# Dilated attention on one core: group sums and weights cross the token orders by way of DRAM, scores and units in pairs

## The chip, the cores and the metric

The kernel runs on one core of a Trainium2 chip. The metric is the time of one execution in microseconds (us), as the device tells it; a run gives the median of its repetitions. TensorE (PE in the profile; PEld is its loading of weights), VectorE (DVE), ScalarE (ACT), GpSimd (POOL) and SyncE (SP) each run their own queue of instructions in order, and wait for one another at semaphores.

## The reference

Two transformer blocks follow each other on 512 tokens of width 1024. The change lies in the second block's first mixer, a dilated attention with 16 heads of 64. Each head attends three times (windows and dilations 128/1, 512/4, 2048/16), and the three results are mixed by a softmax over their log-sums. Cut to what matters:

```python
for g, (window, dilation) in enumerate(DILATED_PATTERNS):     # ((128,1),(512,4),(2048,16))
    q = rotary(proj[:, :, g, 0], pos)
    k = rotary(proj[:, :, g, 1], pos)
    o, lse = dilated_window_attention(q, k, proj[:, :, g, 2], window, dilation)
    outs.append(o); lses.append(lse)
wts = softmax(stack(lses), axis=0)
o = einsum('gbsh,gbshe->bshe', wts, stack(outs))
return o.reshape(B, S, H * E) @ w_out

# in dilated_window_attention, per block of queries
s = where(valid, einsum(q, k) * E**-0.5, -inf)
m = max(s); p = exp(s - m); l = sum(p)
o = einsum(p / l, v); lse = m + log(l)
```

## The kernel before, in words

The weights come as one stream of 328 tiles of 128 x 1024 (`wst`). `Stream` loads a tile on SP's queue (line 170), and splits it into a high part `whi` on ACT (183) and a low part `wlo` on DVE (184); every projection is three fp32r matmuls (260 to 262, or 370 to 372). Loads run two tiles ahead of the splits, splits four tiles ahead of the use.

The attention `attn` works on head pairs `hp`, 0 to 7. `proj(hp)` is a generator that projects q, k and v of one head pair; `att(hp)` is a generator that attends. The loop at its end takes one step of `att(hp-1)` behind each step of `proj(hp)`, so the order of every engine's queue is this interleaving: **a step** in this text is a piece of projection (12 matmuls of 512 columns, or 24 of 256) and the piece of attention behind it. An even `hp` has 20 projection steps, an odd one 16. What `att` has left when `proj` is through follows without projection between. `att(7)` runs beside the output projection `proj_group0`, with two steps of attention to each of its later steps.

Within `att`, before the change: steps 1 to 4 compute scores (657, into PSUM banks named `dn`, of which there are four), each followed by `soft`: maximum with mask on DVE (637), exponential on ACT (641). Group 0 keeps tokens in order, 128 to a block; groups 1 and 2 keep them by residue (token 4p + r). So sums `ML` of group 0 have to change order before the weights `E` of the three groups can be formed: step 5 does that with 16 small fp32 matmuls against the identity (669) and a copy into `ml` (671), and then forms `E` (674 to 685). Step 8 takes group 0's weights back with 16 matmuls against a constant `back` (744) into `c0`. The first two units' probabilities are scaled in step 7. Steps 9 to 17 run over eight **units** (two score blocks of both heads each): transposes on PE (711, 713), a copy of them from PSUM to `PT` (546 on ACT and 548 on DVE, in turns), scaling by weights of the unit two further on (701 for groups 1 and 2, 704 for group 0, both DVE), and the products with v (734) of the unit before. fp32 matmuls of scores, products and weights appear as two records each.

`rots` holds the rotary's second half of each q/k: POOL issues four DMAs that swap rows (585) and multiplies (592); `fin` on DVE multiplies and adds (595, 596) some steps later. POOL's next DMAs wait for `fin` to be through with the buffers `qks` and `qka`, of which there is one each. In the table below "odd" and "even" are the head pair that is projected meanwhile.

Of the kernel before, what the change touches and what calls it, by code (L numbers as in the profile page):

```python
# [26 lines left out]
F32 = mybir.dt.float32  # L27
# [4 lines left out]
OP = mybir.AluOpType  # L32
PSUM = bass.MemoryType.PSUM

S, D = 512, 1024
# [193 lines left out]
class Kern:  # L229
# [287 lines left out]
    def attn(self, ctx):  # L517
        K, nc, tc = self, self.nc, self.tc
        mm = nc.tensor.matmul
        xT = self.xT  # L520
        inner = ExitStack()
        pool = inner.enter_context(tc.tile_pool(name="attn", bufs=1))

        def const(name, shape):
            t = pool.tile(shape, F32, name=name)
            nc.gpsimd.dma_start(t, K.ins["c_" + name])
            return t

        rot = const("rot", [128, 2, S])
        mask0 = const("mask0", [128, 256])  # L530
        mask1 = const("mask1", [128, 128])
        mask2 = const("mask2", [128, 128])
        back = const("back", [128, 4, 128])
        blk = const("blk", [128, 4])
        x_d = self.dr.tile([128, 4, D], F32, name="x_d")
        for tb in range(4):
            nc.gpsimd.dma_start(x_d[:, tb, :], K.x[:, tb, :])
        oT = K.xp.tile([128, 8, S], F32, name="x")
        hT = [None]
        V0, V12, QT = {}, {}, {}  # L540
# [87 lines left out]
        def att(hp):  # L628
            P0 = pool.tile([128, 4, 2, 256], F32, name="P0")
            P12 = [None, pool.tile([128, 4, 2, 128], F32, name="P1"), pool.tile([128, 4, 2, 128], F32, name="P2")]  # L630
            ML = pool.tile([128, 3, 4, 2, 2], F32, name="ML", bufs=2)
# [3 lines left out]
            def soft(items, sl):  # L635
                for s, mk, dst, idx in items:
                    nc.vector.tensor_tensor_reduce(dst, s, mk, op0=OP.add, op1=OP.max, scale=1.0, scalar=-3e38,
                                                   accum_out=M[idx])
                nc.vector.tensor_scalar(NM[sl], M[sl], -0.125, None, op0=OP.mult)
                for s, mk, dst, idx in items:  # L640
                    nc.scalar.activation(dst, dst, AF.Exp, bias=NM[idx], scale=0.125, accum_out=L[idx])  # L641

            A = slice(None)
            for g, t0 in ((0, 0), (0, 2), (1, 0), (2, 0)):
                q = QT[hp, g]
                its = []
                n = 4 if g else 2
                ps = [K.bank("dn", (128, n, 512 // n)) for _ in range(2)]
                for u in range(n):
                    t = t0 + u  # L650
                    c = slice(t * 128, t * 128 + 128)
                    k0 = 128 if g == 0 and t == 0 else 0
                    keys = c if g else slice((t - 1) * 128 + k0, (t + 1) * 128)
                    for h in range(2):
                        r = slice(64 * h, 64 * h + 64)
                        s = ps[h][:, u, k0:]
                        mm(s, q[r, 0, c], q[r, 1, keys], start=True, stop=True)  # L657
                        its.append((s, (mask0, mask1, mask2)[g][:, k0:], (P0, P12[1], P12[2])[g][:, t, h, k0:],
                                    (A, g, t, slice(h, h + 1))))
                soft(its, (A, g, slice(t0, t0 + n)))  # L660
                yield
            for g in range(3):
                del QT[hp, g]

            p = K.bank("dn")
            pv = p[:, 0:16].rearrange("p (r c h) -> p r c h", r=4, c=2)
            for r in range(4):
                for b in range(4):
                    mm(pv[32 * b:32 * b + 32, r], K.ident[:, r:128:4], ML[:, 0, b], start=True, stop=True)
            ml = pool.tile([128, 4, 2, 2], F32, name="ml", bufs=2)  # L670
            nc.vector.tensor_copy(ml, pv)
            E = pool.tile([128, 3, 4, 2], F32, name="E", bufs=2)
            mx = pool.tile([128, 4, 2], F32, name="mx", bufs=2)
            nc.vector.tensor_tensor(mx, M[:, 1], M[:, 2], op=OP.max)
# [8 lines left out]
            nc.vector.tensor_add(mx, mx, T[:, 2])  # L683
            nc.vector.reciprocal(mx, mx)
            nc.vector.tensor_mul(E, E, mx[:, None].to_broadcast([128, 3, 4, 2]))
            Eb = pool.tile([128, 4, 4, 2], F32, name="Eb", bufs=2)
            nc.vector.tensor_mul(Eb, E[:, 0, :, None, :].to_broadcast([128, 4, 4, 2]),
                                 blk[:, None, :, None].to_broadcast([128, 4, 4, 2]))
            units = [(g, t2) for g in (1, 2) for t2 in range(2)] + [(0, b) for b in range(4)]
            c0 = pool.tile([128, 4, 2], F32, name="c0", bufs=2)  # L690
            yield
            yield
            po = K.bank("o")
            PT = {}

            def scale(g, t):
                for h in range(2):
                    if g:
                        for u in (2 * t, 2 * t + 1):
                            s = P12[g][:, u, h, :]  # L700
                            nc.vector.tensor_scalar(s, s, E[:, g, u, h:h + 1], None, op0=OP.mult)
                    else:
                        s = P0[:, t, h, (128 if t == 0 else 0):256]
                        nc.vector.tensor_scalar(s, s, c0[:, t, h:h + 1], None, op0=OP.mult)

            def tr(g, t):
                p = K.bank("dn", (128, 2, 2, 128))
                for u in range(2):
                    for h in range(2):
                        if g:  # L710
                            nc.tensor.transpose(p[:, u, h, :], P12[g][:, 2 * t + u, h, :], K.ident)  # L711
                        elif t or u:
                            nc.tensor.transpose(p[:, u, h, :], P0[:, t, h, u * 128:u * 128 + 128], K.ident)  # L713
                d = pool.tile([128, 2, 2, 128], F32, name="PT", bufs=3)
                u0 = 1 if (g, t) == (0, 0) else 0
                evac(d[:, u0:2], p[:, u0:2])
                PT[g, t] = d
# [3 lines left out]
            def pv_(g, t):  # L721
                d = PT.pop((g, t))
                for u in range(2):
                    if (g, t, u) == (0, 0, 0):
                        continue
                    for h in range(2):
                        if g:
                            c = slice(2 * t + u, S, 4)
                            v = V12[hp][:, 2 * t + u, (g - 1) * 128 + 64 * h:(g - 1) * 128 + 64 * h + 64]
                        else:  # L730
                            c = slice(t * 128, t * 128 + 128)
                            o = (2 * (hp % 2) + h) * 64
                            v = V0[hp // 2][:, t - 1 + u, o:o + 64]
                        mm(po[64 * h:64 * h + 64, c], v, d[:, u, h, :], start=nth[h] == 0, stop=False,  # L734
                           skip_group_check=True)
                        nth[h] += 1

            scale(*units[0])
            scale(*units[1])
            yield  # L740
            pb = K.bank("dn")
            for k in range(4):
                for r in range(4):
                    mm(pb[32 * k:32 * k + 32, 0:8], back[:, r, 32 * k:32 * k + 32], Eb[:, r].rearrange("p b h -> p (b h)"),  # L744
                       start=r == 0, stop=r == 3)
            nc.vector.tensor_copy(c0, pb[:, 0:8].rearrange("p (b h) -> p b h", b=4))
            yield
            for n in range(len(units) + 1):
                if n < len(units):
                    tr(*units[n])  # L750
                if n + 2 < len(units):
                    scale(*units[n + 2])
                if n:
                    pv_(*units[n - 1])
                yield
            if hT[0] is None:
                nc.scalar.activation(oT[:, hp, :], po, AF.Copy)
            else:
                K.split_ps(hT[0][0][:, hp, :], hT[0][1][:, hp, :], po)
# [57 lines left out]
    def mix(self, ctx):  # L817
# [966 lines left out]
def layout(a, stages):  # L1784
    a = {k: np.asarray(v) for k, v in a.items()}
    d = {"x": np.ascontiguousarray(a["x"][0])}
# [13 lines left out]
    d["c_back"] = np.ascontiguousarray(np.stack([j == 4 * (i % 32) + r for r in range(4)], 1).astype(np.float32))  # L1800
    d["c_blk"] = (i // 32 == np.arange(4)[None]).astype(np.float32)
# [51 lines left out]
```

## Time and profile before

| | us |
|---|---|
| times of three runs | 2183.8, 2183.39, 2186.86 (median 2183.8) |
| the profiled execution's own time | 2180.92 |
| its span, first to last instruction | 2179.2 |
| PE busy (share of span) | 2102.1 (96%) |
| PE weight loads busy | 1758.0 (81%) |
| DVE busy | 1223.5 (56%) |
| ACT busy | 794.0 (36%) |
| POOL busy | 272.3 (12%) |
| dilated attention, head pairs 1 to 7 beside `att` | about 690 to 1195 |

The span is one execution seen by the hardware profiler; 1.7 us of its time lie outside. The engines' busy times overlap, and matmuls are pipelined: one of 512 columns is shown 0.39 us long, yet the next begins 0.23 us after it. So what a piece costs PE is read from starts: from the start of the last projection matmul ahead of it to the start of the second one behind it, less two projection intervals. In the stretch 690 to 1110 PE is shown busy throughout, at full granted clock.

### The profile page before, as it was taken

How to read it: one execution, taken by the hardware profiler on the slowest of the kernel's cores; microseconds unless marked ns; L12 is line 12 of the kernel's file. 1: busy time of each engine (PE TensorE's matmuls, PEld its weight loads, DVE VectorE, ACT ScalarE, POOL GpSimd, SP SyncE). 2: the span in 40 equal slices, each digit the busy share in tenths (PEclk: the TensorE clock that was granted, in tenths of full speed). 3: DMA queues.
4: the chain of work that ended last, by engine and by line, in shares of the span. 5: the costliest groups of instructions: out<-in, count | busy, mean ns of one | idle time of the engine just before them, and what ended most of it. 6: DMA issues, size and time to landing. Idle time of an engine off the chain costs nothing.

```text
span 2179.2 us, 31391 instructions
## 1 busy us (share of the span) xinstructions
PE 2102.1 (96%) x12708; PEld 1758.0 (81%) x12708; DVE 1223.5 (56%) x2153; ACT 794.0 (36%) x1470; POOL 272.3 (12%) x327
## 2 busy tenths in 40 slices
PE   5889899999999999999999999999999999999997
PEld 5877698888888888888887988888898878888885
DVE  6876443333466666657766744444556556444444
ACT  5446333222233444333344432223254534322331
POOL 3740100000012222122220100000100001000001
PEclk9999999999999999999999999999999999999998
DMA  3201232222325333333332222223222222222221
GB/s 126 80 23 47 109 126 97 97 90 85 116 102 170 101 100 111 107 96 109 99 116 101 100 100 97 87 87 106 97 91 78 86 78 80 96 96 90 104 97 68
DMA packets 65026, 209.49 MB, mean 96 GB/s; under 512 B 10544, under 2 KB 15312, under 8 KB 64880
## 3 DMA queue, kind: packets, MB, share of 16 engines
q1 hardware_dynamic: 55808, 180.93, 24.1%
q0 software_dynamic: 6928, 20.09, 3.3%
q10 hardware_dynamic: 2144, 6.45, 0.9%
q8 instruction: 100, 1.64, 0.3%
q14 instruction: 46, 0.38, 0.1%
HBM read 186.46 MB, written 4.19 MB: 87 GB/s over the span
## 4 chain that ended last, share of the span: by engine, by line
PE 59%; issue 24%; DVE 2%; POOL 1%; ACT 1%; DMA 0%; POOLq 0%; ACTq 0%; DVEq 0%
PE mm L260 14%; PE mm L261 13%; PE mm L262 13%; PE dn L371 4%; PE dn L370 4%; PE dn L372 4%; PE o L734 1%; PE dn L657 1%; POOL rv L306 1%; POOL rr L308 1%; PE dn L711 1%; PE dn L713 1%; ACT P L641 0%; DVE wlo L184 0%; PE dn L744 0%
## 5 line engine op out<-in xcount | busy, mean ns | idle before, releaser
L260 PE MATMUL mm<-xh,whi 128*128 128x512 f32 (+1 forms) x1488 | 566.7, 381 | 9.0 <-ACT whi L183 5.8
L261 PE MATMUL mm<-xl,whi 128*128 128x512 f32 (+1 forms) x1488 | 558.3, 375 | 2.9 <-DVE xl L313 2.9
L262 PE MATMUL mm<-xh,wlo 128*128 128x512 f32 (+1 forms) x1488 | 558.0, 375 | 0.5 <-DVE wlo L184 0.5
L184 DVE TENSOR_TENSOR wlo<-wst,whi 128x1024 fp32r<-128x1024 f32 x328 | 440.9, 1377 | 137.5 <-ACT whi L183 136.4
L183 ACT ACTIVATE whi<-wst 128x1024 fp32r<-128x1024 f32 x328 | 331.6, 1049 | 350.6 <-PE dn L371 221.7
L260 PEld LDWEIGHTS mm<-xh,whi 128*128 128x128 f32 x1488 | 282.4, 190 | 67.0 <-issue 7.3
L262 PEld LDWEIGHTS mm<-xh,wlo 128*128 128x128 f32 x1488 | 282.7, 190 | 52.2 <-DVE wlo L184 0.8
L261 PEld LDWEIGHTS mm<-xl,whi 128*128 128x128 f32 x1488 | 282.6, 190 | 51.6 <-DVE xl L313 3.9
L371 PE MATMUL dn<-whi,hl 128*128 128x512 f32 x688 | 271.5, 395 | 0.0
L370 PE MATMUL dn<-whi,hh 128*128 128x512 f32 x688 | 270.9, 394 | 0.1
L372 PE MATMUL dn<-wlo,hh 128*128 128x512 f32 x688 | 268.5, 390 | 0.0
L260 PE MATMUL mm<-whi,xh 128*128 128x256 f32 x608 | 178.3, 293 | 1.2 <-DVE kT L1195 1.2
L261 PE MATMUL mm<-wlo,xh 128*128 128x256 f32 x608 | 172.8, 284 | 0.0
L262 PE MATMUL mm<-whi,xl 128*128 128x256 f32 x608 | 172.7, 284 | 0.0
L480 DVE SCALAR_TENSOR_TENSOR x<-x,dn 128x512 f32<-128x512 f32 x112 | 75.6, 685 | 168.8 <-PE dn L372 168.8
L306 POOL TENSOR_SCALAR rv<-ss 128x1 f32<-128x1 f32 (+1 forms) x42 | 26.3, 626 | 1036.0 <-ACT junk L348 440.5
L370 PEld LDWEIGHTS dn<-whi,hh 128*128 128x128 f32 x688 | 129.3, 188 | 30.5 <-DVE x L341 0.5
L372 PEld LDWEIGHTS dn<-wlo,hh 128*128 128x128 f32 x688 | 129.3, 188 | 29.3
L371 PEld LDWEIGHTS dn<-whi,hl 128*128 128x128 f32 x688 | 129.5, 188 | 26.7
L260 PEld LDWEIGHTS mm<-whi,xh 128*128 128x128 f32 x608 | 117.2, 193 | 9.4 <-issue 7.5
L261 PEld LDWEIGHTS mm<-wlo,xh 128*128 128x128 f32 x608 | 117.4, 193 | 0.1
L262 PEld LDWEIGHTS mm<-whi,xl 128*128 128x128 f32 x608 | 117.3, 193 | 0.0
(394 smaller groups left out, 2565.1 us busy)
## 6 DMA issues: line engine op xcount, KB each, us to landing
wst<-in_wstream SPq DMA_DIRECT2D x328, 512.0 KB, 3.6
qks<-qkT POOLq DMA_DIRECT2D x96, 128.0 KB, 2.8
v<-gb SPq DMA_DIRECT2D x128, 32.0 KB, 1.8
X<-in_x SPq DMA_DIRECT2D x4, 512.0 KB, 7.9
xn<-in_x POOLq DMA_DIRECT2D x4, 512.0 KB, 4.6
x_d<-x POOLq DMA_DIRECT2D x4, 512.0 KB, 8.4
x<-x_d POOLq DMA_DIRECT2D x4, 512.0 KB, 7.6
out<-x SPq DMA_DIRECT2D x4, 512.0 KB, 2.6
```

The costliest lines, as they stand in the source:

```text
L183: K.nc.scalar.activation(hi, t, AF.Copy)
L184: K.nc.vector.tensor_sub(lo, t, hi.bitcast(F32))
L260: mm(ps, wh, xh, start=first, stop=False, skip_group_check=True)
L261: mm(ps, wh, xl, start=False, stop=False, skip_group_check=True)
L262: mm(ps, wl, xh, start=False, stop=last, skip_group_check=True)
L306: self.nc.gpsimd.tensor_scalar(v[:, :n], ss, scale, eps, op0=OP.mult, op1=OP.add)
L308: self.nc.gpsimd.tensor_tensor(r[:, :n], v[:, :n], self.nhalf[:, :n], op=OP.pow)
L370: mm(p, hT[i][0][:, c], w[i][0][:, n], start=i == 0, stop=False)
L371: mm(p, hT[i][1][:, c], w[i][0][:, n], start=False, stop=False)
L372: mm(p, hT[i][0][:, c], w[i][1][:, n], start=False, stop=i == m - 1)
L480: nc.vector.scalar_tensor_tensor(x, x, ALPHA if first else 1.0, ps, op0=OP.mult, op1=OP.add)
L657: mm(s, q[r, 0, c], q[r, 1, keys], start=True, stop=True)
```

## The change

- The sums `ML` of group 0 are written to a DRAM tile `ml_d` and read back in the other order into `ml`, both on SP's queue; the 16 matmuls (669) and the copy (671) go. The same for group 0's weights by `c_d` into `c0`: the 16 matmuls (744), the product with `blk` (687) and the copy (746) go, and the constants `back` and `blk` with them.
- Scores of group 0 are computed in one step (eight matmuls, four banks), those of groups 1 and 2 in one step two further on (16 matmuls, four banks). `soft` still takes one half of them a step.
- Units go in pairs: transposes of two units, then products of the two before; the scaling is still one unit a step, one or two steps ahead. `PT` has four buffers, not three.
- `E` is formed in step 6, not 5, and the first pair is scaled there; the first transposes stay in step 9. `att` has 16 yields, not 17.

```diff
+        ml_d = self.dr.tile([S, 4], F32, name="ml_d")
+        c_d = self.dr.tile([S, 2], F32, name="c_d")
...
-            for g, t0 in ((0, 0), (0, 2), (1, 0), (2, 0)):
...
-                soft(its, (A, g, slice(t0, t0 + n)))
...
+            for two in (((0, 0), (0, 2)), ((1, 0), (2, 0))):
+                work = []
+                for g, t0 in two:
...
+                    work.append((its, (A, g, slice(t0, t0 + n))))
+                for n, w in enumerate(work):
+                    soft(*w)
+                    if n == 0:
+                        yield
+                if two[0][0] == 0:
+
+                    nc.sync.dma_start(ml_d.rearrange("(b p) v -> p b v", b=4), ML[:, 0].rearrange("p b c h -> p b (c h)"))
+                    ml = pool.tile([128, 4, 2, 2], F32, name="ml", bufs=2)
+                    nc.sync.dma_start(ml, ml_d.rearrange("(p r) (c h) -> p r c h", r=4, c=2))
                 yield
...
-            for r in range(4):
-                for b in range(4):
-                    mm(pv[32 * b:32 * b + 32, r], K.ident[:, r:128:4], ML[:, 0, b], start=True, stop=True)
-            ml = pool.tile([128, 4, 2, 2], F32, name="ml", bufs=2)
-            nc.vector.tensor_copy(ml, pv)
+            yield
...
+            units = [[(g, t2) for t2 in range(2)] for g in (1, 2)] + [[(0, b), (0, b + 1)] for b in (0, 2)]
             c0 = pool.tile([128, 4, 2], F32, name="c0", bufs=2)
+            nc.sync.dma_start(c_d.rearrange("(p r) h -> p r h", r=4), E[:, 0])
+            nc.sync.dma_start(c0, c_d.rearrange("(b p) h -> p b h", b=4))
+            for u in units[0]:
+                scale(*u)
+            yield
             yield
             yield
...
             for n in range(len(units) + 1):
                 if n < len(units):
-                    tr(*units[n])
-                if n + 2 < len(units):
-                    scale(*units[n + 2])
+                    for u in units[n]:
+                        tr(*u)
                 if n:
-                    pv_(*units[n - 1])
+                    for u in units[n - 1]:
+                        pv_(*u)
+                if n + 1 < len(units):
+                    scale(*units[n + 1][0])
                 yield
+                if n + 1 < len(units):
+                    scale(*units[n + 1][1])
+                    yield
```

How the queues change is seen at three places of the first head pair. In the names, P_5631 and P_5629 are group 1's probabilities (before and after), P_5632 and P_5630 group 2's. First PE, where the products begin, before:

```order
L262 MATMUL mm<-xh,wlo 128x512
L711 MATMUL dn<-ident,P_5632 128x128 x4
L734 MATMUL o<-PT,v_5470 64x128 x4
L260 MATMUL mm<-xh,whi 128x512
L261 MATMUL mm<-xl,whi 128x512
```

and after:

```order
L262 MATMUL mm<-xh,wlo 128x512
L718 MATMUL dn<-ident,P_5630 128x128 x8
L741 MATMUL o<-PT,v_5468 64x128 x8
L260 MATMUL mm<-xh,whi 128x512
L261 MATMUL mm<-xl,whi 128x512
```

Two visits of four transposes and four products have become one of eight and eight. Next DVE, from the weights `E` to the scaling of group 2, before:

```order
L685 TENSOR_TENSOR E<-E,mx 128x24
L687 TENSOR_TENSOR Eb<-E,blk 128x32
L595 TENSOR_TENSOR qks<-qks,rot 128x1024
L596 TENSOR_TENSOR qkT<-qka,qks 128x1024
L701 TENSOR_SCALAR P_5631<-P_5631,E 128x128 x8
L746 COPY c_5826<-dn 128x8
L184 TENSOR_TENSOR wlo<-wst,whi 128x1024 x2
L701 TENSOR_SCALAR P_5632<-P_5632,E 128x128 x4
L548 COPY PT<-dn 128x512
```

and after:

```order
L700 TENSOR_TENSOR E<-E,mx 128x24
L648 TENSOR_SCALAR P_5629<-P_5629,E 128x128 x8
L595 TENSOR_TENSOR qks<-qks,rot 128x1024
L596 TENSOR_TENSOR qkT<-qka,qks 128x1024
L184 TENSOR_TENSOR wlo<-wst,whi 128x1024 x2
L548 COPY PT<-dn 128x512
L648 TENSOR_SCALAR P_5630<-P_5630,E 128x128 x8
L595 TENSOR_TENSOR qks<-qks,rot 128x1024
```

Group 1's scaling now stands ahead of the rotary's `fin` (595, 596), and all eight operations of group 2's scaling stand behind the weight splits and a copy of `PT`. Last SP's queue over the same head pair, before:

```order
L170 DMA wst<-in_wstream 128x1024 x94
L625 DMA v_5470<-gb 32x256 x16
L170 DMA wst<-in_wstream 128x1024 x8
L625 DMA v_6026<-gb 32x256 x16
L170 DMA wst<-in_wstream 128x1024 x10
```

and after:

```order
L170 DMA wst<-in_wstream 128x1024 x2
L679 DMA ml_d<-ML 128x4x4
L681 DMA ml<-ml_d 128x16
L170 DMA wst<-in_wstream 128x1024 x2
L703 DMA c_d<-E 128x8
L704 DMA c_5819<-c_d 128x4x2
L170 DMA wst<-in_wstream 128x1024 x4
```

Four DMAs a head pair, each with a wait of its own, now stand between the loads of the weight stream.

## Rows read from the trace of the kernel before

**Rows 1.** Who PE waited for, 650 to 1150 us: total us, times, longest us

```profile
PE o L734 <- DVE PT L548: 0.8, 3, 0.3
```

**Rows 2.** Timeline of PE around lines 669 and 744: start, length, engine, line, operation

```profile
712.83 0.67 PE L669 MATMUL dn<-ML,ident 128*32 128x4 f32 x32
713.43 0.50 PE L260 MATMUL mm<-xh,whi 128*128 128x512 f32 x1
...
721.50 0.39 PE L262 MATMUL mm<-xh,wlo 128*128 128x512 f32 x1
721.82 0.88 PE L744 MATMUL dn<-Eb,back 128*32 128x8 f32 x32
722.62 0.50 PE L260 MATMUL mm<-xh,whi 128*128 128x512 f32 x1
722.96 0.39 PE L261 MATMUL mm<-xl,whi 128*128 128x512 f32 x1
```

**Rows 3.** Timeline of PE at two steps of scores, group 0 and group 1

```profile
700.74 1.13 PE L657 MATMUL dn<-qkT 64*128 64x256 f32 x8
701.81 0.50 PE L260 MATMUL mm<-xh,whi 128*128 128x512 f32 x1
...
704.75 1.16 PE L657 MATMUL dn<-qkT 64*128 64x128 f32 x16
705.84 0.50 PE L260 MATMUL mm<-xh,whi 128*128 128x512 f32 x1
```

**Rows 4.** Timeline of PE at the first three units of the first head pair

```profile
725.48 0.60 PE L711 MATMUL dn<-ident,P 128*128 128x128 f32 x4
725.84 0.49 PE L260 MATMUL mm<-xh,whi 128*128 128x512 f32 x1
...
728.70 0.60 PE L711 MATMUL dn<-ident,P 128*128 128x128 f32 x4
729.23 0.66 PE L734 MATMUL o<-PT,v 128*64 128x128 f32 x8
729.82 0.50 PE L260 MATMUL mm<-xh,whi 128*128 128x512 f32 x1
...
732.70 0.60 PE L711 MATMUL dn<-ident,P 128*128 128x128 f32 x4
```

**Rows 5.** Timeline of DVE over the same stretch, odd head pair projected

```profile
720.44 0.18 DVE L685 TENSOR_TENSOR E<-E,mx 128x24 f32<-128x24 f32 x1
...
722.16 1.23 DVE L596 TENSOR_TENSOR qkT<-qka,qks 128x1024 f32<-128x1024 f32 x1
723.31 1.71 DVE L701 TENSOR_SCALAR P<-P,E 128x128 f32<-128x128 f32 x8
...
724.95 2.35 DVE L184 TENSOR_TENSOR wlo<-wst,whi 128x1024 fp32r<-128x1024 f32 x2
727.22 3.50 DVE L701 TENSOR_SCALAR P<-P,E 128x128 f32<-128x128 f32 x4
730.64 0.68 DVE L548 COPY PT<-dn 128x512 f32<-128x512 f32 x1
```

**Rows 6.** Timeline of POOL over the same stretch

```profile
723.93 2.02 POOL L585 DMA_DIRECT2D qks<-qkT  x4 [7.58 <-DVE P L701]
725.97 4.08 POOL L592 TENSOR_TENSOR qka<-qkT,rot 128x1024 f32<-128x1024 f32 x1
```

**Rows 7.** Timeline of DVE, even head pair projected, second head pair attended

```profile
784.64 4.82 DVE L184 TENSOR_TENSOR wlo<-wst,whi 128x1024 fp32r<-128x1024 f32 x2 [0.60 <-ACT whi L183]
```

**Rows 8.** DMA issues: engine, count, KB each, median us to landing

```profile
v<-gb SPq DMA_DIRECT2D x128, 32.0 KB, 1.8
...
m_g_ao<-in_g_ao SPq DMA_DIRECT2D x1, 2.0 KB, 3.2
wt<-in_s_b SPq DMA_DIRECT2D x1, 256.0 KB, 8.8
```

**Rows 9.** Timeline of PE beside the output projection, last head pair

```profile
1168.78 0.50 PE L370 MATMUL mm<-whi,xh 128*128 128x512 f32 x1 [1.52 <-DVE x L785]
```

More of the change, by code (lines that the diff above doesn't have):

```diff
@@ L532, in attn @@
         mask2 = const("mask2", [128, 128])
-        back = const("back", [128, 4, 128])
-        blk = const("blk", [128, 4])
         x_d = self.dr.tile([128, 4, D], F32, name="x_d")
+        ml_d = self.dr.tile([S, 4], F32, name="ml_d")
+        c_d = self.dr.tile([S, 2], F32, name="c_d")
         for tb in range(4):
@@ L641, in soft, with scale @@
                     nc.scalar.activation(dst, dst, AF.Exp, bias=NM[idx], scale=0.125, accum_out=L[idx])
-            A = slice(None)
-            for g, t0 in ((0, 0), (0, 2), (1, 0), (2, 0)):
[L645 to L659, printed above, removed]
-                soft(its, (A, g, slice(t0, t0 + n)))
+            def scale(g, t):
+                for h in range(2):
+                    if g:
+                        for u in (2 * t, 2 * t + 1):
+                            s = P12[g][:, u, h, :]
+                            nc.vector.tensor_scalar(s, s, E[:, g, u, h:h + 1], None, op0=OP.mult)
+                    else:
+                        s = P0[:, t, h, (128 if t == 0 else 0):256]
+                        nc.vector.tensor_scalar(s, s, c0[:, t, h:h + 1], None, op0=OP.mult)
@@ new lines, in att @@
+            A = slice(None)
+            for two in (((0, 0), (0, 2)), ((1, 0), (2, 0))):
+                work = []
+                for g, t0 in two:
+                    q = QT[hp, g]
+                    its = []
+                    n = 4 if g else 2
+                    ps = [K.bank("dn", (128, n, 512 // n)) for _ in range(2)]
+                    for u in range(n):
+                        t = t0 + u
+                        c = slice(t * 128, t * 128 + 128)
+                        k0 = 128 if g == 0 and t == 0 else 0
+                        keys = c if g else slice((t - 1) * 128 + k0, (t + 1) * 128)
+                        for h in range(2):
+                            r = slice(64 * h, 64 * h + 64)
+                            s = ps[h][:, u, k0:]
+                            mm(s, q[r, 0, c], q[r, 1, keys], start=True, stop=True)
+                            its.append((s, (mask0, mask1, mask2)[g][:, k0:], (P0, P12[1], P12[2])[g][:, t, h, k0:],
+                                        (A, g, t, slice(h, h + 1))))
+                    work.append((its, (A, g, slice(t0, t0 + n))))
[7 more added lines that the diff above has]
+                    nc.sync.dma_start(ml, ml_d.rearrange("(p r) (c h) -> p r c h", r=4, c=2))
@@ L663, in att @@
                 del QT[hp, g]
-            p = K.bank("dn")
-            pv = p[:, 0:16].rearrange("p (r c h) -> p r c h", r=4, c=2)
-            for r in range(4):
-                for b in range(4):
-                    mm(pv[32 * b:32 * b + 32, r], K.ident[:, r:128:4], ML[:, 0, b], start=True, stop=True)
-            ml = pool.tile([128, 4, 2, 2], F32, name="ml", bufs=2)
-            nc.vector.tensor_copy(ml, pv)
+            yield
             E = pool.tile([128, 3, 4, 2], F32, name="E", bufs=2)
@@ L685, in att @@
             nc.vector.tensor_mul(E, E, mx[:, None].to_broadcast([128, 3, 4, 2]))
[L686 to L689, printed above, removed]
+            units = [[(g, t2) for t2 in range(2)] for g in (1, 2)] + [[(0, b), (0, b + 1)] for b in (0, 2)]
             c0 = pool.tile([128, 4, 2], F32, name="c0", bufs=2)
+            nc.sync.dma_start(c_d.rearrange("(p r) h -> p r h", r=4), E[:, 0])
[3 more added lines that the diff above has]
+            yield
             yield
@@ L694, in att @@
             PT = {}
[L696 to L704, printed above, removed]
             def tr(g, t):
@@ L713, in tr @@
                             nc.tensor.transpose(p[:, u, h, :], P0[:, t, h, u * 128:u * 128 + 128], K.ident)
-                d = pool.tile([128, 2, 2, 128], F32, name="PT", bufs=3)
+                d = pool.tile([128, 2, 2, 128], F32, name="PT", bufs=4)
                 u0 = 1 if (g, t) == (0, 0) else 0
@@ L736, in pv_ @@
                         nth[h] += 1
[L738 to L747, printed above, removed]
             for n in range(len(units) + 1):
                 if n < len(units):
-                    tr(*units[n])
-                if n + 2 < len(units):
-                    scale(*units[n + 2])
+                    for u in units[n]:
+                        tr(*u)
                 if n:
-                    pv_(*units[n - 1])
+                    for u in units[n - 1]:
+                        pv_(*u)
+                if n + 1 < len(units):
+                    scale(*units[n + 1][0])
                 yield
+                if n + 1 < len(units):
+                    scale(*units[n + 1][1])
+                    yield
             if hT[0] is None:
@@ L1799, in layout @@
     d["c_mask2"] = np.where((j <= i) & ((i - j) % 4 == 0), 0, no).astype(np.float32)
-    d["c_back"] = np.ascontiguousarray(np.stack([j == 4 * (i % 32) + r for r in range(4)], 1).astype(np.float32))
-    d["c_blk"] = (i // 32 == np.arange(4)[None]).astype(np.float32)
     d["c_causal64"] = ((i <= j) & (i // 64 == j // 64)).astype(np.float32)
```

## The prediction

> **What bounds the kernel now.** I read the busy times first, then who PE waits for over the attention, then PE's own timeline. PE is busy 96% of the span, and over the attention its recorded waits come to 0.8 us in 500 [rows 1]. So the stage is as long as PE's queue: what is taken from PE's queue is gained, and what makes PE wait is lost. Nothing on DVE, ACT, POOL or SP counts unless PE ends up waiting for it. That makes two questions: how much does PE's queue lose, and which of the slacks that keep PE from waiting are used up?
>
> **What PE loses.** The cost of a visit to the attention is read from starts, as said in the front. Around the 16 matmuls of line 744: the projection matmul ahead starts at 721.50, the second behind at 722.96; less two intervals of 0.23 that is 1.00 us. Of this the way in costs 0.09 (721.82 - 721.50 - 0.23) and the way out 0.11 (722.96 - 722.62 - 0.23) beyond the visit itself. The 16 of line 669 cost 713.43 - 712.83 + 0.09 + 0.11 = 0.80 [rows 2]. Both go: **1.80 us** a head pair. The copies and the product behind them are on DVE and gain nothing by themselves.
>
> Scores: a visit of eight costs 1.27 or 1.29 (start to next projection 1.07 and 1.09, plus 0.20) [rows 3]. Two visits in one save a way in and out (0.20) and most of a slow start and end. From the second row, eight matmuls (16 records) last 1.16 with the last one's own 0.27, so they start 0.13 apart on average; eight more add 0.9 to 1.0 where a visit of their own costs 1.29. Saved 0.3 to 0.4 a pair, two pairs: **0.75**, at the short spacing, since only a visit's first spacing is long.
>
> Units: four transposes alone cost 0.36 + 0.09 = 0.45 (no way in is seen ahead of them), and start 0.11 apart ((0.60 - 0.27) / 3). Four transposes and four products cost 729.82 - 728.70 + 0.10 = 1.22; products start 0.11 apart too, after 0.16 for the first; products alone would cost 0.59 + 0.20 = 0.79 [rows 4]. The first block of tokens has half its keys, so two of the nine visits before are 0.22 shorter. Before: 0.45 + 5 x 1.22 + 2 x 1.00 + 0.79 = 9.34. After, with 0.44 for each further four: 0.89 + 2.10 + 1.88 + 1.88 + 1.23 = 7.98. Saved **1.36**.
>
> Together 3.9 a head pair. I count it for head pairs 0 to 6: 27.4 us. The 0.8 us of waits of [rows 1] belong to last products that follow at once on their transposes; in the new order a projection step lies between, so I add 0.6 (a way in is paid instead). Sum **28.0 us**.
>
> **What PE may wait for now.** Step by step:
>
> Scores of step 3 use four banks, and two of them are read by `soft` in step 2. DVE then has no splits to make (they come in steps 1 and 5), its work in these two steps is what it was, its scores come a step sooner, and no wait for it is recorded before [rows 1]. Nothing, except beside the output projection (below).
>
> The sums by DRAM: on this time axis the second half of group 0's scores came at 700.74 [rows 3] and comes some 2 us sooner now; with its maxima and exponentials I put `ml_d`'s start at about 704.5. `ml` is wanted at about 718, ten small operations ahead of L685's end at 720.6 [rows 5]. Two DMAs at 1.8 to 3.2 us each [rows 8] need 3.6 to 6.4 of 13.5. Nothing. SP stands still meanwhile, and the weight loads behind it with it; but the next load is for a split two takes later, some 10 us on. Nothing; its bound is one load's few us once a head pair, if that cover goes. `c0` is wanted four steps after it is sent: nothing.
>
> First transposes (step 9). `E` is ready at 720.62 before [rows 5]. After, I take 720.1: the copy is gone and ACT's exponentials start some 0.4 sooner. Group 1's eight scalings then take 1.71: 721.8. PE comes to step 9 at 725.48 less 1.80 and 0.75, 722.9. So 1.1 us to spare (about 0.6 when an even head pair is projected, where ACT gains nothing).
>
> Second transposes (step 11): **here a slack goes**. Before, group 2's first scaling was next to the splits, in time by 2 us (730.72 against the transposes at 732.70) although one operation of it took 2.9 us: POOL asked for its multiplication at 725.97, and DVE's operation begun at 727.22 came back when POOL was through, at 730.05 [rows 5, 6]. After, `fin` starts at 721.8 and needs 2.55 (L685's end at 720.62 to L596's end at 723.39, less 0.22 for `blk`): 724.35. The two splits take 2.35 to 726.7, the copy 0.68 to 727.4. POOL's multiplication is asked for 2.58 after `fin` (725.97 - 723.39): 726.9, while the copy runs. It takes 2.9 and DVE stands until 730.3; then all eight scalings of group 2 follow, 1.71: 732.0. PE comes to step 11 at 732.70 - 2.55, plus 0.44 for the fuller step 9, less 1.22 for step 10, which no longer has a visit: 729.4, and to its second half at 729.8. It waits 2.2 us, once a head pair, when an odd one is projected: four times, **8.8 us**. Bounds for it: nothing, if the scalings come first, and 2.9 us each if all of POOL's hold shows.
>
> How sure is the order? The trace shows the split begun at 726.08, 0.11 after POOL asked, still run in its usual 1.2, and only the operation behind it held. So DVE may slip one operation in; the copy is that one. [...]
>
> With an even head pair projected, POOL's multiplication falls earlier, on the splits themselves (4.82 instead of 2.35) [rows 7]; reckoned the same way the scalings end some 0.3 us ahead of the transposes. Nothing, bound 1 us, three times.
>
> **Last head pair.** Beside the output projection PE already waits for DVE: 1.52 us for an addition that frees a bank [rows 9]. Less work on PE is no gain there. The new step 3 waits for the second `soft`, which stands behind two splits there, one visit earlier than the same wait stood before, and the first pair's scaling (1.7) now stands ahead of an addition that frees a bank; against that the waits for 669 and 744 go, and the uncovered end has two visits less. I take 0, with 2 us to either side.
>
> **Sum.** 28.0 - 8.8 = 19.2. The profiled execution of 2180.9 would be 2161.7 (span 2160.0); the median of the runs stood 2.9 above it, and 2183.8 - 19.2 = **2164.6**.
>
> **Rivals.**
> No wait in step 11: POOL's multiplication comes behind the scalings, or DVE comes to them sooner. For it: it needs only that 0.5 us of DVE's queue moves, and DVE runs back to back there. Against: one operation of 2.9 us stands at this place in each of the four such head pairs before. Time 2183.8 - 28 = 2156, with the ends at 2152 to 2159.
>
> More waits: the 0.6 to 1.1 us in step 9 and the 0.3 in step 11 are thin, and ACT's queue sets them. If each head pair loses another 1 us: 2164.6 + 7 = 2172; with 2 us for some, up to 2177.
>
> Slower than before: the round trip to DRAM comes late. DVE then stands at the maximum that reads `ml`, with the weight splits, `fin` and all scalings queued behind it, and PE waits for group 1's transposes, then as before for group 2's. To spare are 13.5 us, then 1 on PE; a head pair has 2.7 left on the mean (19.2 / 7), so it decides from about 17.2 us for the two DMAs, 8.6 each. Against: small ones take 1.8 to 3.2; only at the crowded start did one take 8.8 [rows 8]. At 10 us each they are 6.5 late, 5.5 of it on PE against the 2.7 left: 2.8 lost seven times, 2183.8 + 20 = 2204. [...] No run here shows a 16-byte write to DRAM.
>
> **How the numbers follow.** Chances: forecast 0.52 (2159 to 2169), no wait 0.22, more waits 0.17, slower or no better by late sums 0.09. The range takes in the no-wait case and most of the more-waits case: 2152 to 2175. Runs of this kernel tell about 0.2%, 4.4 us, from no change. Faster by more than that: the first three cases, less a little for waits in several places at once, 0.89. Slower 0.06, within 0.2% 0.05.
>
> **What would show it.** Right: no rows of 669 and 744; visits of eight transposes and eight products of about 2.1 us; one visit in four head pairs with a wait of about 2 us, ended by DVE's scaling of P, with an operation of 2.9 us just ahead of it; `ml` landing well before its maximum is asked for. Wrong: waits of PE in step 3 or step 9, DVE idle until `ml` has landed, or ACT idle ahead of `whi` until a weight load has landed.

## The result and the profile after

| | before | after |
|---|---|---|
| median of the runs on one chip, us | 2185.25 (2183.39 to 2186.86) | **2162.25** (2161.18 to 2164.82) |
| ratio to before | | 0.9899, 95% interval 0.9887 to 0.9911 |
| the profiled execution's own time / span | 2180.92 / 2179.2 | 2164.82 / 2163.0 |
| ahead of the first scores of the attention | 696.94 | 701.19 |
| seven head pairs: first scores of one to first scores of the eighth | 455.87 | **431.87** |
| last head pair: its first scores to the projection matmul behind its last product | 42.12 | **44.49** |
| the rest of the span | 984.22 | 985.5 |

The change gains 23.0 us. The last four lines cut the two profiled spans at rows of PE's timeline. These are the rows, first of the kernel before, then of the changed one (whose first, 701.19, stands further down):

```profile
696.94 0.93 PE L657 MATMUL dn<-qkT 64*128 64x128 f32 x8
...
1152.80 0.93 PE L657 MATMUL dn<-qkT 64*128 64x128 f32 x8
...
1194.93 0.50 PE L370 MATMUL dn<-whi,xh 128*128 128x512 f32 x1
```

```profile
1133.05 1.79 PE L669 MATMUL dn<-qkT 64*128 64x128 f32 x16
...
1177.55 0.50 PE L370 MATMUL dn<-whi,xh 128*128 128x512 f32 x1
```

Ahead of the attention the code is the same but for two constants that are no longer loaded, yet the profiled executions shown here differ there by up to 5 us (one that loads them, `e12_mul_before`, stands at 701.44); so the spans (16.2 us apart) understate the gain, and I compare stage by stage: 24.0 won in seven head pairs, 2.4 lost in the last.

Who PE waited for between 650 and 1150 us, which answers to [rows 1] (total us, times, longest us):

```profile
PE dn L669 <- DVE ML L637: 4.3, 1, 4.3
PE dn L718 <- DVE P L648: 2.5, 4, 0.7
```

The first line is the last head pair. The second is the wait foreseen for step 11: four times, transposes of group 2 that wait for DVE's scaling of P. (In a timeline, a bracket at the end of a row gives the idle time of the engine ahead of the row and what ended it.) PE's timeline, answering to [rows 3] and [rows 4] (line 669 is now the scores, 718 the transposes of groups 1 and 2, 741 the products): a first visit of scores, a second one, the first eight transposes, then step 11 with an even head pair projected and with an odd one:

```profile
700.87 0.39 PE L262 MATMUL mm<-xh,wlo 128*128 128x512 f32 x1
701.19 1.79 PE L669 MATMUL dn<-qkT 64*128 64x128 f32 x16
...
703.24 0.39 PE L261 MATMUL mm<-xl,whi 128*128 128x512 f32 x1
...
708.27 0.39 PE L262 MATMUL mm<-xh,wlo 128*128 128x512 f32 x1
708.59 2.06 PE L669 MATMUL dn<-qkT 64*128 64x128 f32 x32
...
710.91 0.39 PE L261 MATMUL mm<-xl,whi 128*128 128x512 f32 x1
...
726.80 0.40 PE L262 MATMUL mm<-xh,wlo 128*128 128x512 f32 x1
727.04 1.04 PE L718 MATMUL dn<-ident,P 128*128 128x128 f32 x8
...
728.14 0.40 PE L261 MATMUL mm<-xl,whi 128*128 128x512 f32 x1
```

```profile
791.48 0.40 PE L262 MATMUL mm<-xh,wlo 128*128 128x512 f32 x1
791.71 1.04 PE L718 MATMUL dn<-ident,P 128*128 128x128 f32 x8
792.68 1.09 PE L741 MATMUL o<-PT,v 128*64 128x128 f32 x16
...
794.04 0.39 PE L261 MATMUL mm<-xl,whi 128*128 128x512 f32 x1
```

```profile
733.14 0.39 PE L262 MATMUL mm<-xh,wlo 128*128 128x512 f32 x1
734.15 1.72 PE L718 MATMUL dn<-ident,P 128*128 128x128 f32 x8 [0.62 <-DVE P L648]
735.80 1.09 PE L741 MATMUL o<-PT,v 128*64 128x128 f32 x16
...
737.16 0.40 PE L261 MATMUL mm<-xl,whi 128*128 128x512 f32 x1
```

Read as in the prediction (start to start, less two intervals of 0.23), the scores cost 1.91 and 2.18, eight transposes 0.88, eight transposes with eight products 2.10 undisturbed. With the wait the same visit costs 3.56. The bracket shows 0.62 of the 1.46 in between; the rest lies ahead of the row's start and inside it, since the 1.72 of these eight transposes is 1.04 elsewhere: the second four wait again.

### The profile page after: what moved, and what is told of

It reads as the page before. It is cut to its first block, busy times and chain, and to the rows that moved or that the text cites. A ratio compares the mean times of both kernels' runs of the same rounds, so it can differ in the third digit from the quotient of the medians.

```text
span 2163.0 us, 30385 instructions
## 1 busy us (share of the span) xinstructions
PE 2083.6 (96%) x12196; PEld 1759.6 (81%) x12196; DVE 1217.7 (56%) x2129; ACT 793.1 (37%) x1470; POOL 269.7 (12%) x325
## 4 chain that ended last, share of the span: by engine, by line
PE 57%; issue 24%; DVE 3%; POOL 1%; ACT 1%; DMA 1%; POOLq 0%; ACTq 0%; DVEq 0%
PE mm L260 13%; PE mm L261 13%; PE mm L262 13%; PE dn L371 4%; PE dn L370 4%; PE dn L372 4%; PE o L741 1%; PE dn L669 1%; DVE P L648 1%; DVE wlo L184 1%; POOL rv L306 1%; POOL rr L308 1%; PE dn L720 1%; PE dn L718 0%; DMA wst<-in_wstream 0%
## 5 line engine op out<-in xcount | busy, mean ns | idle before, releaser
L184 DVE TENSOR_TENSOR wlo<-wst,whi 128x1024 fp32r<-128x1024 f32 x328 | 436.3, 1363 | 167.0 <-ACT whi L183 165.9
```

Source lines behind the costliest of these rows:

```text
L184: K.nc.vector.tensor_sub(lo, t, hi.bitcast(F32))
```

## Why step 11 waits

DVE and POOL ahead of this visit, answering to [rows 5] and [rows 6]:

```profile
724.41 1.66 DVE L648 TENSOR_SCALAR P<-P,E 128x128 f32<-128x128 f32 x8
...
727.31 1.23 DVE L596 TENSOR_TENSOR qkT<-qka,qks 128x1024 f32<-128x1024 f32 x1
728.45 2.35 DVE L184 TENSOR_TENSOR wlo<-wst,whi 128x1024 fp32r<-128x1024 f32 x2
730.72 0.68 DVE L548 COPY PT<-dn 128x512 f32<-128x512 f32 x1
731.33 4.14 DVE L648 TENSOR_SCALAR P<-P,E 128x128 f32<-128x128 f32 x8
```

```profile
729.08 2.00 POOL L585 DMA_DIRECT2D qks<-qkT  x4 [8.88 <-DVE qkT L596]
731.09 2.91 POOL L592 TENSOR_TENSOR qka<-qkT,rot 128x1024 f32<-128x1024 f32 x1
```

Eight scalings take 1.66 us where nothing is in the way (724.41, group 1's); here 4.14, and the first of them alone took 2.77. POOL's multiplication began at 731.09, in the middle of DVE's copy, and took its 2.91 to 734.00; the scalings that began at 731.33 came through behind it, and PE's transposes at 734.15.

**Experiment: the multiplication on DVE.** The change to the changed kernel:

```diff
-                    nc.gpsimd.tensor_mul(v[0], v[1], tab[0])
                     def fin():
+                        nc.vector.tensor_mul(v[0], v[1], tab[0])
                         nc.vector.tensor_mul(v[2], v[2], tab[1])
```

> The changed kernel with the rotary's first multiplication moved from POOL to DVE, into fin (three times 1.2 us more work on DVE a head pair, none on POOL). If DVE stands still because of POOL, no scaling of P takes 2.9 us any more; the second scaling then ends 2.6 - 1.2 = 1 to 1.4 us sooner, the step 11 wait falls from 1.46 to about 0.5, and seven head pairs take some 428. If DVE's own queue is what makes it late, the further 1.2 us in fin make the wait longer, 2.7 us, and seven head pairs take some 437.

Seven head pairs took 426.0 us (one run, 2155.66), better than the 428 expected, since nothing of the wait is left. DVE now carries 1.2 to 2.0 us more for each multiplication, yet its scalings come in time:

```profile
727.84 2.35 DVE L184 TENSOR_TENSOR wlo<-wst,whi 128x1024 fp32r<-128x1024 f32 x2
730.11 0.68 DVE L548 COPY PT<-dn 128x512 f32<-128x512 f32 x1
730.71 1.65 DVE L647 TENSOR_SCALAR P<-P,E 128x128 f32<-128x128 f32 x8
```

The order of DVE's rows is the one above, the eight scalings take 1.65 again, and no wait of PE for P is left. So POOL's hold of DVE is the cause, and it costs 431.87 - 426.0 = 5.87 us, 1.44 to 1.50 in each of four head pairs (from its first scores to the next one's, 57.91 to 57.97 become 56.47 us in three of them, 54.86 becomes 53.40 in the fourth; the even ones stay at 67.73). The same kernel in four more runs:

> The run e6 again (the changed kernel with the multiplication of L591 on DVE), now timed in rounds for an interval. Theory: 426.0 in the seven head pairs against the changed kernel's 431.9, and 1 to 2 us less in the last: 2155 to 2157 by the median, ratio about 0.987. Rival (the 2155.66 of the single run was a quick one): 2158 or more.

2157.19 us, ratio 0.9871 [0.9854, 0.9887]; seven head pairs 426.0 once more. And the same edit made to the kernel before:

> The kernel before with the multiplication of L591 moved from POOL to DVE, and nothing else. Theory (before the change the hold falls where PE has slack, so it costs nothing there): seven head pairs 455.9 as before, within 0.5, and a time within 0.2% of the kernel before. Rival (DVE as such is relieved by the move, whatever the change does): seven head pairs 450 or less, the same 5.9 us as between the changed kernel and e6.

2186.63 in one run, seven head pairs 455.83: nothing. The hold was there before the change as well [rows 5, 6], under slack; the change used the slack up. That settles the rival that taking POOL's hold off DVE is worth something by itself.

**Experiment: group 2 scaled together with group 1.** The other way out is to bring the scalings ahead of POOL's request:

```diff
-            for u in units[0]:
+            for u in units[0] + (units[1] if hp < 7 else []):
                 scale(*u)
...
```

(and the two scalings of group 2 behind step 9 left out).

> The changed kernel with group 2's scaling taken up to step 6, right behind group 1's, ahead of the rotary's fin, the weight splits and POOL's multiplication (for head pairs 0 to 6; the others of the pairs' scalings keep their steps). If the wait in step 11 (0.62 to 0.65 us shown ahead of the first transpose and 0.85 inside, 1.46 in all, four times) comes from the scaling standing behind POOL's hold, it goes: seven head pairs at 431.9 - 5.8 = 426.1, the time 5 to 6 us below the changed kernel's. If it only moves, to PT's copy or to step 9, under half of this.

2161.16, ratio 0.9892 [0.9877, 0.9907]; seven head pairs 430.03, not 426.1: a miss. Step 11 is free, but step 13 waits, for the weights of group 0. In the seven head pairs DVE waited for the swapped rows of q and k 2.1 us in all in the changed kernel, and here:

```profile
DVE qks L595 <- DMA qks<-qkT: 17.8, 4, 4.6
```

DVE's timeline and PE's in such a head pair:

```profile
737.45 2.02 DVE L595 TENSOR_TENSOR qks<-qks,rot 128x1024 f32<-128x1024 f32 x1 [4.47 <-DMA qks<-qkT]
...
741.32 1.00 DVE L651 TENSOR_SCALAR P<-P,c 128x128 f32<-128x128 f32 x4
```

```profile
741.74 0.43 PE L720 MATMUL dn<-ident,P 128*128 128x128 f32 x2 [0.45 <-DVE P L651]
```

The eight further scalings stand ahead of `fin` now, so `fin` ends 1.6 us later, and POOL's four DMAs that swap rows, which need `fin`'s buffer, go out at 730.65 instead of 729.08. They land at 737.4; the next `fin` waits for them, and group 0's scalings stand behind that `fin`. DVE stood idle for 4.47 us with scalings queued behind the wait. What was freed in one visit was lost in the next by 1.0 us a time ((430.03 - 426.0) / 4).

## Which part gave what

Three kernels, each the kernel before with one part of the change.

**Sums and weights by DRAM alone**: the 16 + 16 matmuls, `back`, `blk` and `Eb` out; the four DMAs on `ml_d` and `c_d` in, at the places they have in the change.

```diff
+                    nc.sync.dma_start(ml_d.rearrange("(b p) v -> p b v", b=4), ML[:, 0].rearrange("p b c h -> p b (c h)"))
+                    nc.sync.dma_start(ml, ml_d.rearrange("(p r) (c h) -> p r c h", r=4, c=2))
...
-                    mm(pv[32 * b:32 * b + 32, r], K.ident[:, r:128:4], ML[:, 0, b], start=True, stop=True)
...
-                    mm(pb[32 * k:32 * k + 32, 0:8], back[:, r, 32 * k:32 * k + 32], Eb[:, r].rearrange("p b h -> p (b h)"),
```

> The kernel before with the DRAM round trips alone: 669, 671, 687, 744 and 746 go, scores and units stay single. From the first scores of head pair 0 to those of head pair 7 the kernel before needs 455.9 us, the changed one 431.9; from there to the end of the attention 42.1 and 44.5. If PE's queue is what counts, seven head pairs lose 1.80 us each: 443.3, with no wait of PE in them; the last head pair changes by under 2 us, and the time is some 12 to 14 us below before. The rival, that the trip through DRAM itself costs time, expects DVE to stand at the maximum that reads ml, PE to wait for the scaled P, and under half of that gain.

**Scores in pairs alone**:

```diff
-            for g, t0 in ((0, 0), (0, 2), (1, 0), (2, 0)):
+            for two in (((0, 0), (0, 2)), ((1, 0), (2, 0))):
...
```

> The kernel before with the scores in pairs alone. Queue theory: each pair saves one way in and out, 0.35 to 0.4 us, so seven head pairs take 455.9 - 5.4 = 450.5, and no PE wait in them. The last head pair should show by itself what the changed kernel showed: PE waits about 4 us ahead of group 2's scores for DVE's maxima, and its stretch grows from 42.1 by 1 to 3 us. So 2 to 5 us below before in all. The rival, that the last head pair's loss came from the DRAM trip, expects its stretch at 42 here.

**Units in pairs alone**:

```diff
-            units = [(g, t2) for g in (1, 2) for t2 in range(2)] + [(0, b) for b in range(4)]
+            units = [[(g, t2) for t2 in range(2)] for g in (1, 2)] + [[(0, b), (0, b + 1)] for b in (0, 2)]
...
```

> The kernel before with the units in pairs alone, the matmuls 669 and 744 kept, group 1 scaled in step 7 behind the rotary. Queue theory: 1.4 us a head pair, 455.9 - 10 = 446, and little or no wait in step 11, since PE comes there some 2.5 us later than in the changed kernel while DVE's and POOL's work is the same (under 0.3 us a time). The rival, that pairing the units by itself makes PE wait for the second scaling, expects the same 1.5 us four times: 452.

| | median us | ratio | seven head pairs | saved | forecast | last head pair |
|---|---|---|---|---|---|---|
| before | 2185.25 | | 455.87 | | | 42.12 |
| DRAM alone | 2174.68 | 0.9949 [0.9932, 0.9965] | 443.26 | 12.61 | 7 x 1.80 = 12.6 | 42.83 |
| scores alone | 2183.83 | 0.9991 [0.9982, 1.0] | 450.15 | 5.72 | 7 x 0.75 = 5.25 | 45.25 |
| units alone | 2172.07 | 0.9938 [0.9923, 0.9953] | 444.69 | 11.18 | 7 x 1.36 + 0.6 = 10.1 | 41.24 |
| all three (after) | 2162.25 | 0.9899 [0.9887, 0.9911] | 431.87 | 24.00 | 19.2 | 44.49 |

(Each ratio is to the kernel before as it ran beside that kernel.) The parts save 29.5 one by one and 24.0 together. The missing 5.5 is step 11's wait, which none of them has alone: with any one of them DVE's slack there still suffices. POOL's hold is there in each of them (the longest scaling takes 2.9, 2.9 and 2.35 us in the table's order), and PE waits for none. Without the wait (the multiplication on DVE) the three together save 29.9, the sum of the parts and 0.4 more. The units are the plainest case: among PE's waits in that run, 640 to 1200 us, none is for a scaling of P.

The scores in pairs, worth 5.7 in seven head pairs, give 3.1 back in the last: by the medians they are hardly to be told from no change.

## Is the round trip hidden?

**A second round trip** behind the first, so that `ml` comes by four DMAs instead of two:

```diff
+                    m1 = pool.tile([128, 4, 4], F32, name="m1", bufs=2)
+                    nc.sync.dma_start(m1, ml_d.rearrange("(b p) v -> p b v", b=4))
+                    nc.sync.dma_start(ml_e.rearrange("(b p) v -> p b v", b=4), m1)
...
-                    nc.sync.dma_start(ml, ml_d.rearrange("(p r) (c h) -> p r c h", r=4, c=2))
+                    nc.sync.dma_start(ml, ml_e.rearrange("(p r) (c h) -> p r c h", r=4, c=2))
```

> The changed kernel with the sums sent through DRAM twice (written, read, written to a second DRAM tile, read again). The trip took 3.6 + 1.7 us where DVE asked for ml 8.6 us after it had landed, so the theory that it is hidden expects seven head pairs at 431.9 within 0.5 us, and only the last head pair longer, by the second trip, 3 to 6 us. The theory that SP's standing still delays the weight stream expects PE or ACT to wait for weight tiles in every head pair, and 435 us or more.

2166.53 (one run). Seven head pairs 431.88: a whole further trip costs nothing there. The issues of the changed kernel's trip in the first head pair (length of the issue in ns, first and last start; then the times to landing of the two together), and when DVE asks for `ml`:

```profile
L679 SPq DMA_DIRECT2D ml_d<-ML x1: 388/388/388, 708.6 to 708.6; - x1
L681 SPq DMA_DIRECT2D ml<-ml_d x1: 333/333/333, 712.2 to 712.2; - x1
...
DMA to landing us min/median/max: 1.8/2.7/3.6
```

```profile
722.53 0.17 DVE L690 TENSOR_TENSOR mx<-mx,ml 128x8 f32<-128x8 f32 x1
```

The write landed after 3.6 us, the read after 1.8, at 714.0; DVE asked 8.5 us later and did not stand. In the last head pair the second trip does show: that stage takes 48.5 instead of 44.49.

## The last head pair

The changed kernel beside the output projection, PE and DVE:

```profile
1140.54 1.16 PE L669 MATMUL dn<-qkT 64*128 64x128 f32 x16
1146.01 2.42 PE L669 MATMUL dn<-qkT 64*128 64x128 f32 x16 [4.31 <-DVE ML L637]
...
1159.54 0.50 PE L370 MATMUL mm<-whi,xh 128*128 128x512 f32 x1 [1.77 <-DVE x L787]
```

```profile
1142.57 2.36 DVE L184 TENSOR_TENSOR wlo<-wst,whi 128x1024 fp32r<-128x1024 f32 x2
1144.85 0.41 DVE L637 CUSTOM_DVE_ANT_0 P<-dn,mask 128x256 f32<-128x256 f32 x1
...
1155.35 0.17 DVE L690 TENSOR_TENSOR mx<-mx,ml 128x8 f32<-128x8 f32 x1 [3.81 <-DMA ml<-ml_d]
```

Two things are late. Group 2's scores need the banks of group 0's second half; DVE reads these only from 1144.85 on, behind two splits of weights (and DVE had stood 2.45 us for ACT until 1140.58), and PE stands 4.31 us. Then DVE stands 3.81 us until `ml` has landed, and the additions that free PE's banks stand behind it: 1.77 us at 1159.54, which answers to the 1.52 of [rows 9]. In this stretch the write took 5.1 us, the longest of the eight:

```profile
L679 SPq DMA_DIRECT2D ml_d<-ML x1: 378/378/378, 1148.6 to 1148.6; - x1
L681 SPq DMA_DIRECT2D ml<-ml_d x1: 326/326/326, 1153.8 to 1153.8; - x1
...
DMA to landing us min/median/max: 1.5/3.3/5.1
```

The one-part kernels tell which edit costs what here: the pairing of scores 45.25 - 42.12 = 3.1, DRAM 0.7, the units a gain of 0.9; summed 45.1, measured 44.49. How much of it is the waits themselves, and how much the lower clock in this stage (0.51 and 0.52 of full speed in two stretches of the changed kernel, last section), they do not tell.

**Scores one visit at a time, in the last head pair only:**

```diff
-            for two in (((0, 0), (0, 2)), ((1, 0), (2, 0))):
+            pairs = (((0, 0), (0, 2)), ((1, 0), (2, 0)))
+            for two in pairs if hp < 7 else tuple((x,) for p in pairs for x in p):
...
```

> The changed kernel with the last head pair's scores one group a step, as before the change. If the 4.3 us wait ahead of group 2's scores is the pairing's (both halves' banks wanted at once), it goes, the low clock behind it too, and the last head pair's stretch falls from 44.5 to about 42; seven head pairs stay at 431.9. The rival, that DVE's lateness beside the output projection sets the stretch whatever the scores do, expects the wait to come back ahead of another instruction and the stretch to stay over 43.5.

2163.19, ratio 0.9901 [0.9885, 0.9916]; last head pair 43.9, not about 42: as its rival had it, the wait came back ahead of another instruction and the stage stayed over 43.5. The 4.3 us wait is gone and another has come:

```profile
PE mm L370 <- DVE x L788: 6.0, 2, 4.5
```

DVE still stood 3.49 us for `ml`, with an addition that frees a bank queued behind it, and PE, which came sooner, waited for that. The two late things overlap: with the first away the second shows.

**Two steps of the attention ahead of the output projection instead of one** (on top of group 2's early scaling):

```diff
-            if hp == 4:
+            if hp in (4, 5):
                 a = step(a)
...
```

> The early scaling, and for the last head pair two steps of attention, not one, between the splits ahead of the output projection, so that the second half of the scores' maxima stands ahead of the weight splits on DVE. The wait ahead of group 2's scores should fall from 4.3 to 1 or 2 us, and the steps left uncovered at the end are one fewer: the last head pair at 40 to 42 us, seven head pairs at 426, the time some 8 to 10 us below the changed kernel's. If ACT's queue takes DVE's place there (the splits' copies behind more exponentials), the stretch stays near 44.

2162.75, ratio 0.9896 [0.988, 0.9913]; last head pair 44.84: a miss again. (So are the seven head pairs, 431.6 for 426: the early scaling loses as above, and PE waited 3.5 us for group 0's scaling, the longest time 2.0, where it was 1.9 and 0.7.) The wait for the scores' banks fell to 2.0, and a bank for the projection came 5.6 late:

```profile
PE mm L370 <- DVE x L789: 5.6, 1, 5.6
...
PE dn L669 <- DVE ML L637: 2.0, 1, 2.0
```

**Both causes away, and the multiplication on DVE.** In the last head pair the scores come singly and `ml` by the 16 matmuls of before; all other head pairs are as in the changed kernel with the multiplication on DVE.

```diff
+            if hp == 7:
+                p = K.bank("dn")
+                pv = p[:, 0:16].rearrange("p (r c h) -> p r c h", r=4, c=2)
+                for r in range(4):
+                    for b in range(4):
+                        mm(pv[32 * b:32 * b + 32, r], K.ident[:, r:128:4], ML[:, 0, b], start=True, stop=True)
+                ml = pool.tile([128, 4, 2, 2], F32, name="ml", bufs=2)
+                nc.vector.tensor_copy(ml, pv)
+            else:
+                yield
...
```

> The changed kernel with the multiplication of L591 on DVE (as in the run e6), and in the last head pair the scores one visit at a time and the sums of group 0 by 16 matmuls of PE, as before the change. Theory (POOL's hold of DVE is the whole of the waits in step 11, and the last head pair loses by the pairing of its scores and by the round trip, which comes back too late there): seven head pairs 426.0 as in e6, the last head pair 41 to 42 as in e3, so about 2154 by the medians. Rival (the last head pair loses to something else in the change, for instance the units in pairs or the DRAM trip of the weights): last head pair stays at 43 to 44.5, time about 2156 to 2157, no different from e6 alone.

**2151.59 us** (2149.98 to 2154.43), ratio **0.9849 [0.9835, 0.9864]**: faster than both kernels, by 33.6 us than the kernel before run beside it (2185.14) and by 10.7 than the changed one, which ran at another time (the intervals of the two ratios do not meet). Seven head pairs 426.0, the last 41.10. Of PE's waits, 640 to 1200 us, the longest left is that of [rows 9]:

```profile
PE mm L370 <- DVE x L796: 1.8, 2, 1.5
...
```

So with both late things away the last head pair is 1.0 shorter than before the change. Of the 3.4 us between 44.49 and 41.10, 1.6 came already with the multiplication on DVE (42.91 and 42.79 in its two profiled runs, with a wait of 4.4 for the banks still there). About 1.1 of it is the wait for the additions (0.7 and 0.6 for 1.77); where the rest lies, and how the multiplication brings it about, I have not followed. The other 1.8 came with two edits made at once, and is not split between them.

## Why the prediction came out right, and where its sizes were off

Forecast 2164.6 (2152 to 2175, faster), measured 2162.25. The gain was forecast at 19.2 and measured at 23.0; the times lie closer than that, since the kernel before stands at 2185.25 beside the change, and the forecast started from 2183.8. By its own steps:

- **What PE loses.** 1.80 for the sums and weights: 1.80 (12.61 / 7). Scores 0.75: 0.82. Units 1.36, or 1.45 with the waits that go: 1.60. In all 28.0 forecast for seven head pairs; 24.0 + 5.87 = 29.9 measured. The method, starts around a visit at full clock, holds to 7%.
- **The wait in step 11.** Place, cause, and count were right: odd head pairs alone, four times, behind an operation of POOL of 2.9 us. The size was not: 1.46 for 2.2, 5.87 for 8.8. The step that failed is "the copy is that one": I let POOL begin when DVE's copy ends. It began at once, 0.31 us before that (731.09 against 731.40). Counted from the stage's start, POOL began at 29.9 us (30.5 forecast), PE came to the visit at 32.2 (32.5 forecast), the scalings ended at 34.3 (35.1 forecast): 0.56 of these 0.8 us is POOL's earlier begin, the rest that one of the eight scalings was through with POOL's hold and only seven followed (1.47 us, not 1.71). And in the kernel before I had read the split at 726.08 as slipped in; POOL's row there is 4.08 long instead of 2.91, which reads as POOL waiting for that split. Across the copy in the changed kernel POOL took 2.91. What sets the copy apart from the split was not tried.
- **Nothing in steps 3 and 9, the trip hidden.** Right: no such wait in seven head pairs, 8.5 us to spare for `ml`. Its two DMAs, put at 3.6 to 6.4 us, together took 5.4 us in the first head pair and 6.6 in the last.
- **The last head pair, 0 within 2 us.** Wrong: it lost 2.4. I named the two late things (the second `soft` behind two splits; bank-freeing additions later) and set the visits that go against them. The one-part kernels show that the pairing's side outweighs: 3.1 lost by the scores against 0.2 won by the other two parts. That the trip to DRAM would be late here I did not see: its 13.5 us to spare are the steady state's, where a step of projection lies between the visits, and here the write took 5.1 us.
- **The sum.** 29.9 - 5.9 - 2.4 = 21.6 against 19.2: the wait sized too long by 2.9 and PE's work too short by 1.9 outweigh the 2.4. That these cancel in part is luck, and so is that the time came out closer (2.35 off) than the gain (3.8 off), by the kernel before standing 1.45 higher. The medians say 23.0, their ratio's interval 19.4 to 24.7; the 1.4 between 21.6 and 23.0 I cannot place in a stage.
- **The slower rival** was far off: even four DMAs were hidden. The no-wait rival (2156) is what the multiplication on DVE gives: 2157.19.

## What to carry to other kernels

When a change takes work from the engine that sets the time, list the slack of every engine that feeds it at each point: the gain is what is left when the first of these slacks runs out, and a small operation on a third engine (2.9 us on POOL) may decide which. Parts that are free one by one (no wait of step 11 in any) cost 5.5 us together here, so a sum of single parts can overstate the whole. And a stage's end without cover wants its own plan: a trip to DRAM and a wider visit, both hidden in seven head pairs here, showed in the last (DVE stood 3.81 us, PE 4.31), which runs beside other work.

## What the runs showed of the hardware that I had not expected

- A write of 8 KB to DRAM, by the edit 512 pieces of 16 bytes (539 packets under 512 B from 708.4 to 712.3), landed after 2.8 us in the median, 3.6 in the first head pair and 5.1 in the last; the 4 KB of `c_d`, 128 pieces of 32 bytes (144 packets from 724.4 to 725.8), after 1.4. Count, KB each and median us to landing, in the changed kernel:

```profile
ml_d<-ML SPq DMA_DIRECT2D x8, 8.0 KB, 2.8
...
c_d<-E SPq DMA_DIRECT2D x8, 4.0 KB, 1.4
```

  The 5.1 fell where the 16 DMA engines were busy 68% (1148.64 to 1153.75); whether that is the reason was not tried.
- In the last head pair TensorE's granted clock fell to 0.50 of full speed for some us, twice in the changed kernel: from about 1143.6 to 1150.4, beginning while PE stood still for 4.31 us, and from about 1160.7 to 1164.1, beginning about 1 us after the wait of 1.77. By stretch, with the granted clock as the third number from the end:

```profile
1140.50:1143.50 3.00, 1.20 (x17) 0.97 (x16) 2.83 (x4) 2.98 (x5) 0.47 (x1) 1.00 0.07 21
1143.50:1150.50 7.00, 4.49 (x21) 3.88 (x22) 6.93 (x44) 3.96 (x19) 1.71 (x4) 0.51 0.86 299
...
1160.50:1164.00 3.50, 3.50 (x11) 2.57 (x10) 0.00 (x0) 0.00 (x0) 0.00 (x0) 0.52 0.34 128
```

  Scores in the first of the two falls came 0.15 apart (2.42 for 16) where they took 1.16 before, and projection matmuls in the second started 0.43 apart instead of 0.23, so PE loses time there beyond the waits. From such rows the two falls cost PE an estimate of 3.7 us (1.3 for the 16 scores, 0.9 and 1.5 for five and eight projection matmuls), more than the 2.4 that the last head pair lost. Whether the waits bring it about stays open: in the kernel of 2151.59 projection matmuls start 0.43 apart from 1139.24 to 1142.64, right behind a wait of 1.52 (granted clock 0.83 over 1137 to 1147); in the kernel before, behind a wait of 1.52 as well, the granted clock is 1.00 over 1135 to 1200.
